# Attention of a hybrid backbone block: head loop rewritten as slots in a fixed order, with side work in a list of jobs

## The chip, the cores and the metric

The kernel runs on one core of a Trainium2 chip. The metric is the device time of one execution in microseconds, the median of the runs. The engines of the core are named as the profile names them: PE (matrix multiplies), PEld (its weight loads), DVE (vector), ACT (scalar), POOL (GpSimd), SP (issues the DMAs).

## The reference, cut to what matters

Two streams, 512 latent tokens `x` and 256 context tokens `ctx`, pass through two layers with shared weights; width is 1024, the FFN is 2816 wide. Layer 0 mixes by differential attention, layer 1 by a gated short convolution; each layer ends in a SwiGLU FFN. Only the latent stream is returned, so the context stream is needed in layer 0 alone, as keys and values. What the change touches is the attention:

```python
def diff_attention(h, hc, wqkv, lam, subln_g, wo, cos, sin, layer_idx, need_ctx):
    # 8 heads; each has two maps of 64 channels (q, k) and 128 value channels
    q, k, v = project(h)
    q, k = apply_rope_2d(q, cos, sin), apply_rope_2d(k, cos, sin)
    qc, kc, vc = project(hc)
    k_all, v_all = concat(kc, k), concat(vc, v)          # 768 keys
    s = einsum('bqhmd,bkhmd->bhmqk', qb, k_all) * 64 ** -0.5
    p = softmax(s)                                        # for each map m
    p = p[:, :, 0] - lam_full * p[:, :, 1]
    o = einsum('bhqk,bkhe->bqhe', p, v_all)
    return (rmsnorm(o, subln_g) * (1 - lam_init)).reshape(B, n, D_MODEL) @ wo
```

around it stand `x + g1 * y` with the gate `g1` from `silu(c) @ ada_w[i] + ada_b[i]`, and the FFN `x + g2 * swiglu(modulate(rmsnorm(x), sh2, sc2))`.

## The kernel before

All operands of a multiply are split in a high and a low part (`split`, L53: ACT writes the rounded part, DVE the rest), and a product is three matmuls on PE: high by high, high by low, low by high (`mm3`, L77 to L80). A weight block is loaded by SP into `raw`, split into `whi`/`wlo` (`load_w`, L64), and then used.

The kernel has an opening stage (norm of the inputs, adaLN of the first sub-layer, and the projections of head 0, ending at about 87 us), attention with its output projection (to 437 us), the FFN of layer 0, the convolution, and the FFN of layer 1. The order on each engine comes from a planner (`schedule_with_timeline_sim`) which moves instructions ahead of others by modelled times; the program gives the dependences.

In attention, `finish_q` and `finish_k` (L442, L451) turn a projection into operands. `rope` (L418) copies PSUM to SBUF on ACT, shuffles on DVE, and does two products and a sum on POOL (for head 0 on DVE). The result is split into `qt`/`kt`, and `halves_to` (L432) moves the halves by eight DMAs a head through SP, so that `ks[m]` holds the high part of 64 channels on partitions 0 to 63 and the low part on 64 to 127, and `qs[m]` the high (or low) part twice. One matmul of 128 rows then gives two of the partial products at once, and two passes give four.

`attend` (L508) goes over a head's four query blocks of 128. For each it computes scores of both maps (`S`, L528: for each map two 512-wide and two 256-wide matmuls), the row maximum on DVE (L532), the exponential on ACT (L536), mixes the maps on DVE (L546), transposes the 768 probabilities on PE (`pt`, L551) and splits them (`pth`, `ptl`). After two blocks the product with the values (`po`, 18 matmuls of 256 columns) follows. `subnorm` (L567) is the norm of a head's output, with its square and its diagonal tiles on POOL. The other work of the loop comes from lists: `proj_qk_steps` and `proj_v_steps` (projections of the next heads), `ada_steps` (L361: the gate and shifts of later sub-layers; ACT scales a 128x1024 block, POOL adds it, L374), and `wo_steps` (L649: output projection of the first `NA` = 5 heads, `poa`). After the loop `wo_rest` (L674) adds the other 3 heads (`pob`) for each half of the tokens, `norm_half` makes the FFN's input, and FFN matmuls (`pa`) begin.

PSUM: two `S` tiles of 1024 columns, two `acc` tiles (projections) and two `pt` tiles (transposes, values, norms).

Of the kernel before, what the change touches and what calls it, by code (L numbers as in the profile page):

```python
# [11 lines left out]
F32 = mybir.dt.float32  # L12
# [7 lines left out]
EPS = 1e-6  # L20
LAM_INIT = 0.8 - 0.6 * math.exp(-0.3 * 0)
# [3 lines left out]
def block_kernel(  # L25
# [87 lines left out]
    early = ("ada", "araw", "qt", "kt", "rcos", "rsin", "sw", "rt")  # L113
# [7 lines left out]
    for tag, n, bufs in (  # L121
        [(f"Or{h}", 512, 1) for h in range(NH)] + [("qs0", 1024, 2), ("qs1", 1024, 2)]
        + [("e", 768, 3), ("pth", 768, 3), ("ptl", 768, 3), ("ks0", 768, 2), ("ks1", 768, 2)]
        + [(f"v{p}{t}", 256, 2) for t in range(KB) for p in "hl"]
        + [("sq", 512, 1), ("dg0", 512, 1), ("dg1", 512, 1)]
        + [(t, 4, 2) for t in ("sv", "sr", "rh", "rl")] + [(t, 4, 3) for t in ("rr", "mx")] + [("ss", 8, 2), ("den", 8, 2)]
        + [("ld", 2, 1)]
        + [("araw", 1024, 2), ("ada", 1024, 1), ("qt", 1024, 1), ("kt", 1536, 1), ("rcos", 512, 1), ("rsin", 512, 1)]
        + [("sw", 512, 1), ("rt", 512, 2)]
    ):  # L130
        ap.tile([P, n], F32, tag=tag, bufs=bufs, name=f"place_{tag}")
# [7 lines left out]
    st1, st2 = (ap.tile([P, P], F32, tag=t, name=n) for t, n in (("ks1", "st1"), ("ks1", "st2")))  # L139
# [20 lines left out]
    def nat(src, t, tag, bufs, name):  # L160
# [6 lines left out]
          for t, (tag, bufs) in enumerate((("ada", 1), ("qt", 1), ("qs0", 2), ("qs0", 2)))]  # L167
    raws0.append(load_ada0(0, 1))
    cn = [nat(ctx, t, "qs1", 2, f"cn{t}") for t in range(CB)]
# [37 lines left out]
    def nat_rstd(src, tag, name):  # L207
# [16 lines left out]
        o = ap.tile([P, 512], F32, tag=tag, bufs=2 if tag == "ks0" else 1, name=f"rs{name}")[:, :nb * P]  # L224
# [51 lines left out]
    rc = nat_rstd(cn, "ks0", "c")  # L276
# [14 lines left out]
    for k in range(DB):  # L291
        raws = raws0 if k == 0 else [load_ada0(k, hf) for hf in range(2)]
        raw = ap.tile([P, 512], F32, tag="e", bufs=3, name=f"raw_w0_{k}")
# [31 lines left out]
    nc.sync.dma_start(rsin, rope_sin)  # L325
# [35 lines left out]
    def ada_steps(l, j, pool, ps_pool, spread_sum):  # L361

        acc = pool.tile([P, D], F32, tag="ada", bufs=1, name=f"ada{l}_{j}")
        for k in range(DB):
            raw = pool.tile([P, D], F32, tag="araw", name=f"araw{l}_{j}_{k}")
            nc.sync.dma_start(raw, ada_w[l, k * P:(k + 1) * P, j * D:(j + 1) * D])
            s = sil[:, 0, k:k + 1]
            if not spread_sum:
# [3 lines left out]
                else:  # L372
                    nc.scalar.activation(raw, raw, AF.Copy, scale=s)
                    nc.gpsimd.tensor_tensor(acc, acc, raw, op=ALU.add)  # L374
# [7 lines left out]
        if not spread_sum:  # L382
            ps = ps_pool.tile([P, 512], F32, tag="acc", name=f"pada{l}_{j}")[:, :DB]
# [32 lines left out]
    SWAP = [i ^ 16 for i in range(32)]  # L416
# [24 lines left out]

    def finish_q(h, ps):  # L442

        r = rope(ps, HD ** -0.5, f"q{h}")
        qt = ap.tile([P, 2, T], F32R, tag="qt", bufs=1, name=f"qt{h}")
        split(qt[:, 0, :], qt[:, 1, :], r)
        q = [ap.tile([P, 2, T], F32R, tag=f"qs{m}", name=f"qs{h}_{m}") for m in range(2)]
        halves_to(q, qt, True)
        return q

    def finish_k(h, ps, psc):  # L451

        r = rope(ps, None, f"k{h}")
        kt = ap.tile([P, 2, KV], F32R, tag="kt", bufs=1, name=f"kt{h}")
        split(kt[:, 0, T:], kt[:, 1, T:], psc)
        split(kt[:, 0, :T], kt[:, 1, :T], r)
        ks = [ap.tile([P, KV], F32R, tag=f"ks{m}", name=f"ks{h}_{m}") for m in range(2)]
        halves_to(ks, kt, False)
        return ks

    def finish_v(g, t, ps):
        vh = ap.tile([P, 256], F32R, tag=f"vh{t}", name=f"vh{g}_{t}")
        vl = ap.tile([P, 256], F32R, tag=f"vl{t}", name=f"vl{g}_{t}")
        split(vh, vl, ps)
        return vh, vl

    def v_load(g):
        cols = slice(2 * D + 256 * g, 2 * D + 256 * (g + 1))
        return [load_w(da_wqkv[0, a * 512:(a + 1) * 512, cols], f"wv{g}_{a}") for a in range(2)]

    def v_tile(g, t, ws):
        src, o = (hx, t * P) if t < TB else (hc, (t - TB) * P)
        ps = psB.tile([P, 512], F32, tag="acc", name=f"psv{g}_{t}")[:, :256]
        for k in range(DB):
            wh, wl = ws[k // 4]
            mm3(
                ps, src[k][0][:, o:o + P], src[k][1][:, o:o + P], wh[:, k % 4, :], wl[:, k % 4, :],
                k == 0, k == DB - 1,
            )
        return finish_v(g, t, ps)  # L480

    V, Q, K = {}, {}, {}
    XT, O = [], []
    NA = NH - 3

    def proj_qk_steps(h):
        wq = load_w(da_wqkv[0, :, P * h:P * (h + 1)], f"wq{h}")
        yield
        wk = load_w(da_wqkv[0, :, D + P * h:D + P * (h + 1)], f"wk{h}")
        ps = psB.tile([P, 512], F32, tag="acc", name=f"psq{h}")  # L490
        gemm_block(ps, [wq], hx)
        Q[h] = finish_q(h, ps)
        yield
        ps = psB.tile([P, 512], F32, tag="acc", name=f"psk{h}")
        gemm_block(ps, [wk], hx)
        psc = psB.tile([P, 512], F32, tag="acc", name=f"pskc{h}")[:, :C]
        gemm_block(psc, [wk], hc)
        K[h] = finish_k(h, ps, psc)
        yield

    def proj_v_steps(g, ts):
        ws = v_load(g)
        yield
        for t in ts:
            V.setdefault(g, []).append(v_tile(g, t, ws))
            yield

    def attend(h, between, after=None):  # L508
        q, ks, vs = Q[h], K[h], V[h // 2]
        vc = slice((h % 2) * P, (h % 2) * P + P)  # L510
        O = ap.tile([P, T], F32, tag=f"Or{h}", bufs=1, name=f"O{h}")
        den = ap.tile([P, 2, TB], F32, tag="den", name=f"den{h}")
        for pr in range(2):
            pts = []
            for kh in range(2):
                pts.append(
                    (ap.tile([P, 3, 256], F32R, tag="pth", bufs=3, name=f"pth{h}_{pr}_{kh}"),
                     ap.tile([P, 3, 256], F32R, tag="ptl", bufs=3, name=f"ptl{h}_{pr}_{kh}"))
                )
            for s in range(2):  # L520
                qb = 2 * pr + s
# [439 lines left out]
```

## Time and profile before

| | |
|---|---|
| Median of 3 runs | 1371.86 us (1370.03 to 1374.06) |
| Profiled execution: own time, span | 1369.84 us, 1368.1 us |
| PE busy over the span | 1312.1 us (96%) |
| DVE, ACT, POOL busy | 780.4, 529.6, 244.8 us |
| Opening stage, 0 to 87 us: PE busy | 67.0 us |
| Attention, 87 to 437 us: PE, DVE busy | 325.6 us, 271.1 us |
| Rest, 437 to 1368 us: PE busy | 919.5 us of 931 |

PE's busy time counts a matmul from its start to its modelled end, and consecutive matmuls overlap, so the distance from one start to the next tells what a matmul costs in a stream. The clock column of a window is the granted clock of PE as a share of full speed (2.4 GHz); it has two levels, 1.0 and 0.5.

### The profile page before, as it was taken

How to read it: one execution, taken by the hardware profiler on the slowest of the kernel's cores; microseconds unless marked ns; L12 is line 12 of the kernel's file. 1: busy time of each engine (PE TensorE's matmuls, PEld its weight loads, DVE VectorE, ACT ScalarE, POOL GpSimd, SP SyncE). 2: the span in 40 equal slices, each digit the busy share in tenths (PEclk: the TensorE clock that was granted, in tenths of full speed). 3: DMA queues.
4: the chain of work that ended last, by engine and by line, in shares of the span. 5: the costliest groups of instructions: out<-in, count | busy, mean ns of one | idle time of the engine just before them, and what ended most of it. 6: DMA issues, size and time to landing. Idle time of an engine off the chain costs nothing.

```text
span 1368.1 us, 18008 instructions
## 1 busy us (share of the span) xinstructions
PE 1312.1 (96%) x7052; PEld 1128.1 (82%) x7052; DVE 780.4 (57%) x1043; ACT 529.6 (39%) x872; POOL 244.8 (18%) x197
## 2 busy tenths in 40 slices
PE   6889899899999999999999999999999999999997
PEld 4678799798888988888888889888988888888887
DVE  6886976777886766776753255444473333332322
ACT  6655646454555432333222244222362232232222
POOL 3244635524314100000001041000340000000000
PEclk9999999999999999999999999999999999999999
DMA  8957633623432666666643333333333333333321
GB/s 291 271 151 219 189 101 124 152 80 93 135 97 80 197 206 200 219 222 203 212 128 96 100 93 93 93 98 88 92 93 99 102 92 93 106 91 109 94 78 62
DMA packets 238742, 182.79 MB, mean 134 GB/s; under 512 B 6937, under 2 KB 220226, under 8 KB 238658
## 3 DMA queue, kind: packets, MB, share of 16 engines
q1 hardware_dynamic: 238658, 181.65, 44.7%
q8 instruction: 55, 0.90, 0.3%
q14 instruction: 29, 0.24, 0.1%
HBM read 162.75 MB, written 4.19 MB: 122 GB/s over the span
## 4 chain that ended last, share of the span: by engine, by line
PE 79%; DVE 8%; DMA 4%; ACT 4%; issue 2%; POOL 2%; SPq 0%; DVEq 0%; ACTq 0%; POOLq 0%
PE po_fo L78 6%; PE po_fo L79 6%; PE po_fo L80 6%; PE pb L79 5%; PE pb L78 5%; PE pb L80 5%; PE pa L78 5%; PE pa L79 5%; PE pa L80 5%; DMA araw<-in_ada_w_dram 3%; PE S L528 2%; PE psc L79 1%; PE psb L80 1%; PE psu L80 1%; PE psc L80 1%
## 5 line engine op out<-in xcount | busy, mean ns | idle before, releaser
L54 ACT CAST whi_f<-raw_f 128x1024 fp32r<-128x1024 f32 x87 | 91.4, 1051 | 234.6 <-issue 117.9
L55 DVE TENSOR_TENSOR wlo_f<-raw_f,whi_f 128x1024 fp32r<-128x1024 f32 x87 | 107.4, 1234 | 79.2 <-ACT whi_f L54 76.2
L55 DVE TENSOR_TENSOR wlo_fo<-raw_fo,whi_fo 128x1024 fp32r<-128x1024 f32 (+1 forms) x48 | 54.5, 1135 | 118.4 <-ACT whi_fo L54 116.8
L607 POOL TENSOR_TENSOR nacc<-nacc,nsq 128x256 f32<-128x256 f32 x30 | 30.7, 1023 | 494.1 <-ACT nsq L603 493.6
L78 PE MATMUL po_fo<-uh,whi_fo 128*128 128x512 f32 (+1 forms) x324 | 118.8, 367 | 0.1
L79 PE MATMUL po_fo<-ul,whi_fo 128*128 128x512 f32 (+1 forms) x324 | 118.7, 366 | 0.0
L80 PE MATMUL po_fo<-uh,wlo_fo 128*128 128x512 f32 (+1 forms) x324 | 118.6, 366 | 0.0
L54 ACT CAST whi_fo<-raw_fo 128x1024 fp32r<-128x1024 f32 (+1 forms) x48 | 47.1, 981 | 177.6 <-PE po_fo L79 146.9
L378 DVE SCALAR_TENSOR_TENSOR ada<-araw,sil,ada 128x1024 f32<-128x1024 f32 x49 | 62.9, 1284 | 39.0 <-DMA araw<-in_ada_w_dram 38.7
L803 DVE TENSOR_TENSOR uu<-sl,pb 128x512 f32<-128x512 f32 (+1 forms) x48 | 30.7, 640 | 81.5 <-PE pb L80 77.2
L536 ACT ACTIVATE e<-S,mx 128x768 f32<-128x768 f32 x64 | 57.8, 904 | 46.7 <-DVE mx L532 36.1
L80 PE MATMUL pb<-h2h,wlo_f 128*128 128x512 f32 (+1 forms) x192 | 71.8, 374 | 0.0
L78 PE MATMUL pa<-h3h,whi_f 128*128 128x512 f32 (+1 forms) x192 | 71.6, 374 | 0.0
L79 PE MATMUL pb<-h2l,whi_f 128*128 128x512 f32 (+1 forms) x192 | 71.5, 372 | 0.0
L78 PE MATMUL pb<-h2h,whi_f 128*128 128x512 f32 (+1 forms) x192 | 71.4, 372 | 0.0
L78 PE MATMUL pb<-h3h,whi_f 128*128 128x512 f32 (+1 forms) x192 | 71.4, 372 | 0.0
L79 PE MATMUL pb<-h3l,whi_f 128*128 128x512 f32 (+1 forms) x192 | 71.4, 372 | 0.0
L80 PE MATMUL pa<-h3h,wlo_f 128*128 128x512 f32 (+1 forms) x192 | 71.4, 372 | 0.0
L80 PE MATMUL pb<-h3h,wlo_f 128*128 128x512 f32 (+1 forms) x192 | 71.4, 372 | 0.0
L79 PE MATMUL pa<-h3l,whi_f 128*128 128x512 f32 (+1 forms) x192 | 71.2, 372 | 0.0
L78 PEld LDWEIGHTS po_fo<-uh,whi_fo 128*128 128x128 f32 x324 | 61.2, 189 | 10.1 <-DVE on L890 0.3
L79 PEld LDWEIGHTS po_fo<-ul,whi_fo 128*128 128x128 f32 x324 | 61.1, 189 | 9.9
(362 smaller groups left out, 3715.2 us busy)
## 6 DMA issues: line engine op xcount, KB each, us to landing
raw_f<-in_ffn_w_in_dram SPq DMA_DIRECT2D x88, 512.0 KB, 3.6
araw<-in_ada_w_dram SPq DMA_DIRECT2D x80, 512.0 KB, 4.4
raw_fo<-in_ffn_w_out_dram SPq DMA_DIRECT2D x32, 512.0 KB, 3.7
raw_a<-in_ada_w_dram SPq DMA_DIRECT2D x32, 256.0 KB, 4.6
qs<-qt SPq DMA_DIRECT2D x32, 256.0 KB, 4.9
raw_wv<-in_da_wqkv_dram SPq DMA_DIRECT2D x12, 512.0 KB, 5.0
ks<-kt SPq DMA_DIRECT2D x32, 192.0 KB, 4.8
raw_fo<-in_ffn_w_out_dram SPq DMA_DIRECT2D x16, 384.0 KB, 4.0
```

The costliest lines, as they stand in the source:

```text
L54: nc.scalar.copy(hi, src)
L55: nc.vector.tensor_tensor(lo, src, hi.bitcast(F32), op=ALU.subtract)
L78: nc.tensor.matmul(ps, sh, mh, start=start, stop=False)
L79: nc.tensor.matmul(ps, sh, ml, start=False, stop=False)
L80: nc.tensor.matmul(ps, sl, mh, start=False, stop=stop)
L378: nc.vector.scalar_tensor_tensor(acc, raw, s, acc, op0=ALU.mult, op1=ALU.add)
L528: nc.tensor.matmul(S[:, a:b], q[m][:, j, qb * P:(qb + 1) * P], ks[m][:, a:b], start=(j == 0), stop=(j == 1),)
L536: nc.scalar.activation(em, S[:, :KV], AF.Exp, bias=mx[:, m:m + 1], accum_out=den[:, m, qb:qb + 1])
L607: nc.gpsimd.tensor_tensor(acc, acc, sq, op=ALU.add)
L803: nc.vector.tensor_tensor(u, s, pb, op=ALU.mult)
```

## The change

Order. PE, DVE, ACT and POOL get a fixed order from the end of the opening stage to the end of the first half of `pob`: what the program says in sequence is what each engine does in sequence (`manual_schedule`). The unit is a slot, one query block of one head; there are 32. In slot i: maxima and exponentials of i, side work, transposes of block i - 1, the mix of i, side work, every second slot the values product, then the scores of block i + 1. `fill(us)` issues that much PE work from one list (`beside_softmax`: 17 projection tasks, then 8 tasks of the output projection); `spot(dve, act)` issues stages of waiting jobs (rope, splits) up to that much time on each engine. A job whose result is needed is issued in full at that point (`finish`).

Scores. The DMAs of `halves_to` are gone. Each map's 64 channels stay where the projection left them, map 0 on partitions 0 to 63 and map 1 on 64 to 127, and scores are three matmuls of 64 rows for each map and width, the two maps in turn: 12 matmuls a block instead of 8.

Rope. Four DVE operations that read PSUM (the sine table is shuffled once ahead), none on ACT or POOL.

Others. POOL's additions in `ada_steps` are halved in width, and the block is fetched a step ahead; the square in `subnorm` goes from POOL to ACT; `NA` is 6; before the first scores four stretches of projections of head 1 are issued; `sqrt_ahead` comes after the fixed part.

```diff
-    nc.sync.dma_start(rsin, rope_sin)
+    rsw = ap.tile([P, T], F32, tag="sw", name="rsw", bufs=1)
+    nc.sync.dma_start(rsw, rope_sin)
+    nc.vector.stream_shuffle(rsin, rsw, SWAP)
...
+                    for hf in range(2):
+                        cs = slice(hf * 512, hf * 512 + 512)
+                        nc.gpsimd.tensor_tensor(acc[:, cs], acc[:, cs], raw[:, cs], op=ALU.add)
...
-    def rope(ps, scale, name):
-        eng = nc.vector if name in ("q0", "k0") else nc.gpsimd
-        r = ap.tile([P, T], F32, tag="rt", name=f"rt{name}")
-        s = ap.tile([P, T], F32, tag="sw", bufs=1, name=f"sw{name}")
-        if scale is None:
-            nc.scalar.copy(r, ps)
-        else:
-            nc.scalar.activation(r, ps, AF.Copy, scale=scale)
-        nc.vector.stream_shuffle(s, r, SWAP)
-        eng.tensor_tensor(r, r, rcos, op=ALU.mult)
-        eng.tensor_tensor(s, s, rsin, op=ALU.mult)
-        eng.tensor_tensor(r, r, s, op=ALU.add)
-        return r
...
-    def halves_to(dst, src, both):
-        for m in range(2):
-            s = src[64 * m:64 * m + 64]
-            for d in range(2):
-                o = dst[m][64 * d:64 * d + 64]
-                nc.sync.dma_start(
-                    o.bitcast(F32), (s if both else s[:, d, :]).bitcast(F32)
-                )
...
+    class Job:
...
+        def finish(self, left=0):
+            while len(self.stages) > left:
+                self.step()
+    def spot(*room):
+        room = list(room)
+        for job in list(jobs):
+            eng = job.stages[0][0]
+            while job.stages and job.stages[0][0] == eng and room[eng] > 0.1:
+                room[eng] -= job.stages[0][1]
+                job.step()
+    def split_stages(hi, lo, src, us):
+        get = src if callable(src) else lambda: src
+        return [
+            (ACT, us, lambda: nc.scalar.copy(hi, get())),
+            (DVE, us, lambda: nc.vector.tensor_tensor(lo, get(), hi.bitcast(F32), op=ALU.subtract)),
...
+    def acc_tile(name):
+        if len(taken) > 1:
+            job, left = taken[-2]
+            job.finish(left)
+        taken.append(None)
+        return psB.tile([P, 512], F32, tag="acc", name=name)
...
+    def rope(ps, name):
+        made = {}
+        def first():
+            for job in ropes[:-1]:
+                job.finish()
+            del ropes[:-1]
+            ropes.append(made["job"])
+            made["r"] = ap.tile([P, T], F32, tag="rt", name=f"rt{name}")
+            made["b"] = ap.tile([P, T], F32, tag="sw", bufs=1, name=f"sw{name}")
+            nc.vector.tensor_tensor(made["b"], ps, rsin, op=ALU.mult)
+        def shuffle():
+            made["t"] = ap.tile([P, T], F32, tag="tmp", bufs=1, name=f"tmp{name}")
+            nc.vector.stream_shuffle(made["t"], made["b"], SWAP)
+        return made, [
+            (DVE, 0.7, first),
+            (DVE, 0.7, lambda: nc.vector.tensor_tensor(made["r"], ps, rcos, op=ALU.mult)),
+            (DVE, 0.75, shuffle),
+            (DVE, 0.7, lambda: nc.vector.tensor_tensor(made["r"], made["r"], made["t"], op=ALU.add)),
...
+        made["job"] = done_q[h] = Job(stages + [
+            (ACT, 0.6, lambda: nc.scalar.activation(hi, made["r"], AF.Copy, scale=HD ** -0.5)),
+            (DVE, 0.9, lambda: nc.vector.scalar_tensor_tensor(
+                lo, made["r"], HD ** -0.5, hi.bitcast(F32), op0=ALU.mult, op1=ALU.subtract)),
+        ])
...
+    WIDE, NARROW = 0.68, 0.36
+    def task_k(h):
+        def run(ws):
+            wh, wl = ws[0]
+            ps = acc_tile(f"psk{h}")
+            for k in range(DB):
+                mm3(ps, wh[:, k, :], wl[:, k, :], *hx[k], k == 0, k == DB - 1)
+                yield WIDE
+            read_by(job_k(h, ps), 4)
+            psc = acc_tile(f"pskc{h}")[:, :C]
+            for k in range(DB):
+                mm3(psc, wh[:, k, :], wl[:, k, :], *hc[k], k == 0, k == DB - 1)
+                yield NARROW
+            read_by(job_kc(h, psc), 0)
...
+        fetch(0)
+        fetch(1)
+        begin_split(0)
+        for n, (_, run) in enumerate(tasks):
+            job, ws = ready.pop(n)
+            job.finish()
+            begin_split(n + 1)
+            fetch(n + 2)
+            yield from run(ws)
...
+    def scores(i):
+        h, qb = divmod(i, TB)
+        begun.add(h)
+        out = [psB.tile([P, 1024], F32, tag="S", name=f"S{h}_{qb}_{m}") for m in range(2)]
+        for a, b in ((0, 512), (512, KV)):
+            for j, (jq, jk) in enumerate(((0, 0), (0, 1), (1, 0))):
+                for m in range(2):
+                    r = slice(64 * m, 64 * m + 64)
+                    nc.tensor.matmul(
+                        out[m][:, a:b], Q[h][r, jq, qb * P:(qb + 1) * P], K[h][r, jk, a:b],
+                        start=(j == 0), stop=(j == 2),
+                    )
+        return out
...
+        nc.scalar.activation(sq, O, AF.Square)
+        yield
...
+    beside_softmax = in_turn(
+        [task_k(1), task_q(1), task_v(1), task_k(2), task_q(2), task_k(3), task_q(3), task_v(2), task_k(4), task_q(4),
+         task_k(5), task_q(5), task_k(6), task_q(6), task_v(3), task_k(7), task_q(7)]
+        + [task_wo(k) for k in range(DB)] + [task_wob()]
+    )
...
+    def fill(us):
+        nonlocal owed
+        owed += us
+        while owed > 0:
+            got = next(beside_softmax, None)
+            if got is None:
+                owed = 0.0
+                return
+            owed -= got
...
+    with tc.manual_schedule(engines={
...
+        taken += [(job_q(0, qps), 4), (job_k(0, kps), 4)]
+        job_kc(0, kcps)
+        for t in range(KB):
+            job_v(0, t, vps[t // TB][:, (t % TB) * 256:(t % TB + 1) * 256])
+        for _ in range(4):
+            fill(3.0)
+            spot(2.8, 2.0)
+        for job in done_k[0] + [done_q[0]] + done_v[0]:
+            job.finish()
+        S, e, ready = scores(0), None, None
+        for i in range(NH * TB):
...
+            part = 2.5 if h < NH - 1 else 2.2
...
+            mix = soften(i, S)
+            spot(1.2, 0.4)
+            fill(part)
+            if i:
+                turn(i - 1, e)
+                if qb % 2 == 0:
+                    ready = divmod((i - 1) // 2, 2)
+            e = mix()
             next(adas, None)
...
+            spot(3.4, 3.6)
+            fill(part)
+            one_step()
+            if h == NH - 1:
+                one_step()
+            if ready:
+                values(*ready)
+                after_values(*ready)
+                ready = None
+            if i + 1 < NH * TB:
+                hn = (i + 1) // TB
+                while hn not in done_q:
...
+                for job in done_k[hn] + [done_q[hn]]:
+                    job.finish()
...
+                S = scores(i + 1)
+        fill(2.5)
+        turn(NH * TB - 1, e)
+        one_step()
+        spot(3.0, 3.0)
+        fill(2.0)
+        one_step()
+        values(NH - 1, 1)
+        after_values(NH - 1, 1)
+        fill(100)
...
+        split_out(NH - 2, 0, T).finish()
+        while len(later) > 1:
+            one_step()
+        for k in range(0, DB, 2):
+            one_step()
+            for kk in (k, k + 1):
+                wo_block(psB, kk, *halves[0])
+        while later:
+            one_step()
...
+    sqrt_ahead(0)
```

## Rows read from the trace of the kernel before

**Rows 1.** Page of the profile: span, and busy time with share and instructions of each engine.

```profile
span 1368.1 us, 18008 instructions
...
PE 1312.1 (96%) x7052; PEld 1128.1 (82%) x7052; DVE 780.4 (57%) x1043; ACT 529.6 (39%) x872; POOL 244.8 (18%) x197
```

**Rows 2.** Windows by stage: PE, PEld, DVE, ACT, POOL busy us (x), clock, DMA share, GB/s.

```profile
60.00:87.00 27.00, 23.27 (x145) 19.84 (x143) 21.21 (x31) 14.34 (x22) 11.86 (x5) 0.87 0.65 203
87.00:108.00 21.00, 17.21 (x94) 14.34 (x93) 16.59 (x22) 10.09 (x17) 13.82 (x7) 1.00 0.54 148
108.00:405.00 297.00, 279.36 (x1763) 252.02 (x1764) 231.88 (x366) 160.28 (x307) 125.35 (x82) 0.97 0.47 131
405.00:437.00 32.00, 29.01 (x218) 26.74 (x216) 22.59 (x45) 16.22 (x36) 14.91 (x21) 1.00 0.26 83
```

**Rows 3.** Timeline of PE in a dense stretch: start us, us, engine, line, operation, tiles.

```profile
268.82 0.39 PE L79 MATMUL psk<-hl,whi_wk 128*128 128x512 f32 x1
269.04 0.40 PE L80 MATMUL psk<-hh,wlo_wk 128*128 128x512 f32 x1
269.28 0.49 PE L551 MATMUL pt<-ident,e 128*128 128x128 f32 x3
269.52 0.48 PE L78 MATMUL psk<-hh,whi_wk 128*128 128x512 f32 x1
...
271.13 0.86 PE L528 MATMUL S<-ks,qs 128*128 128x512 f32 x4
271.83 0.28 PE L79 MATMUL pskc<-cl,whi_wk 128*128 128x256 f32 x1
271.95 0.28 PE L80 MATMUL pskc<-ch,wlo_wk 128*128 128x256 f32 x1
```

**Rows 4.** Groups of DVE, 108 to 405 us: count, busy, mean ns, idle before, releaser.

```profile
L532 DVE TENSOR_REDUCE mx<-S 128x1 f32<-128x768 f32 x64 | 60.2, 948 | 13.9 <-PE S L528 13.8
L546 DVE SCALAR_TENSOR_TENSOR e<-e,rr,e 128x768 f32<-128x768 f32 x31 | 40.7, 1312 | 0.6
L55 DVE TENSOR_TENSOR ptl<-pt,pth 128x384 fp32r<-128x384 f32 x60 | 32.2, 549 | 11.7 <-ACT pth L54 11.7
...
L55 DVE TENSOR_TENSOR wlo_wq<-raw_wq,whi_wq 128x1024 fp32r<-128x1024 f32 x5 | 10.3, 2053 | 0.4 <-ACT whi_wq L54 0.4
...
L55 DVE TENSOR_TENSOR wlo_wk<-raw_wk,whi_wk 128x1024 fp32r<-128x1024 f32 x6 | 7.3, 1223 | 4.3 <-ACT whi_wk L54 4.3
...
L426 DVE STREAM_SHUFFLE swk<-rtk 128x512 f32<-128x512 f32 x7 | 5.2, 743 | 0.0
```

**Rows 5.** Groups of ACT in the same stretch, same columns.

```profile
L536 ACT ACTIVATE e<-S,mx 128x768 f32<-128x768 f32 x64 | 57.8, 904 | 46.7 <-DVE mx L532 36.1 <-DVE e L546 9.8 <-DVE vl L55 0.4
L54 ACT CAST pth<-pt 128x384 fp32r<-128x384 f32 x60 | 28.2, 480 | 30.8 <-PE pt L551 30.3
...
L536 ACT ACTIVATION_READ_ACCUMULATOR e<-S,mx 128x1 f32 x64 | 12.6, 197 | 0.0
```

**Rows 6.** Timeline of DVE, then POOL, at the end of the opening stage.

```profile
64.52 2.88 DVE L230 SCALAR_TENSOR_TENSOR na<-XT,A,rsx 128x512 f32<-128x512 f32 x1
...
71.40 0.75 DVE L230 SCALAR_TENSOR_TENSOR na<-XT,A,rsx 128x512 f32<-128x512 f32 x1
...
85.91 0.42 DVE L55 TENSOR_TENSOR vl<-vps,vh 128x256 fp32r<-128x256 f32 x1 [4.62 <-ACT vh L54]
...
89.95 0.68 DVE L428 TENSOR_TENSOR swq<-swq,rsin 128x512 f32<-128x512 f32 x1
...
63.50 3.34 POOL L374 TENSOR_TENSOR ada<-ada,araw 128x1024 f32<-128x1024 f32 x1 [0.46 <-ACT araw L373]
```

**Rows 7.** Waits, 108 to 405 us: waiter <- releaser, us in total, times, longest.

```profile
PE psv L78 <- DVE kt L55: 5.7, 1, 5.7
```

**Rows 8.** Timeline of all engines: end of attention, first FFN matmul.

```profile
425.71 0.48 DVE L640 SCALAR_TENSOR_TENSOR XR<-pob,mod,XR 128x256 f32<-128x256 f32 x1 [0.60 <-PE pob L80]
...
437.27 0.47 PE L78 MATMUL pa<-h2h,win 128*128 128x256 f32 x1
```

More of the change, by code (lines that the diff above doesn't have):

```diff
@@ L20 @@
 EPS = 1e-6
+SWAP = [i ^ 16 for i in range(32)]
 LAM_INIT = 0.8 - 0.6 * math.exp(-0.3 * 0)
@@ L451, in finish_k, with __init__, step @@
[L451 to L461, printed above, removed]
+    DVE, ACT = 0, 1
+    jobs = []
+    class Job:
+        def __init__(self, stages, after=None):
+            self.stages, self.after = list(stages), after
+            jobs.append(self)
+        def step(self):
+            self.stages.pop(0)[2]()
+            if not self.stages:
+                jobs.remove(self)
+                if self.after:
+                    self.after()
+        def finish(self, left=0):
+            while len(self.stages) > left:
+                self.step()
@@ new lines, in block_kernel, with read_by @@
+    taken = []
+    def acc_tile(name):
[4 more added lines that the diff above has]
+        return psB.tile([P, 512], F32, tag="acc", name=name)
+    def read_by(job, left):
+        taken[-1] = (job, left)
+    ropes = []
+    def rope(ps, name):
[16 more added lines that the diff above has]
+            (DVE, 0.7, lambda: nc.vector.tensor_tensor(made["r"], made["r"], made["t"], op=ALU.add)),
+        ]
@@ new lines, in job_q @@
+    def job_q(h, ps):
+        q = ap.tile([P, 2, T], F32R, tag="q", name=f"q{h}")
+        made, stages = rope(ps, f"q{h}")
+        hi, lo = q[:, 0, :], q[:, 1, :]
+        Q[h] = q
+        made["job"] = done_q[h] = Job(stages + [
[3 more added lines that the diff above has]
+        ])
+        return done_q[h]
@@ L672, in block_kernel, with split_out, task_wo, run @@
-    wob = []
+    split_o = {}
+    def split_out(h, a, b):
+        return Job(split_stages(O[h][0][:, a:b], O[h][1][:, a:b], On[h][:, a:b], 0.7 * (b - a) / T))
+    def task_wo(k):
+        def run(ws):
+            if k == 0:
+                h_pool.release()
+                for nm in ("xtp", "op"):
+                    pools.append(tc.alloc_tile_pool(name=nm, bufs=1, side="right", reuse_waits="tile"))
+                for b in range(DB):
+                    XT.append(pools[0].tile([P, T], F32, name=f"XR{b}"))
+                    nc.sync.dma_start(XT[b], xt_dram[b])
+                for h in range(NH):
+                    O.append(pair(pools[1], h, f"o{h}"))
+            wh, wl = ws[0]
+            ps = acc_tile(f"poa{k}")
+            for h in range(NA):
+                while h not in normed_heads:
+                    yield None
+                for ahead in (h, h + 1):
+                    if ahead < NA and ahead in normed_heads and ahead not in split_o:
+                        split_o[ahead] = split_out(ahead, 0, T)
+                split_o[h].finish()
+                mm3(ps, wh[:, h, :], wl[:, h, :], *O[h], h == 0, h == NA - 1)
+                yield WIDE
+            read_by(Job([(DVE, 0.75, lambda: residual(ps, k, 0, 2, 0, T))]), 0)
+        return lambda: [fetch_w(da_wo[0, :NA * P, P * k:P * (k + 1)], f"woa{k}")], run
@@ L674, in wo_rest, with task_wob, run, wo_block @@
+    wob = []
+    def task_wob():
+        def run(ws):
+            wob.extend(ws)
+            yield 0.0
+        return lambda: [fetch_w(da_wo[0, h * P:(h + 1) * P, :], f"wob{h}") for h in range(NA, NH)], run
+    def wo_block(pool, k, a, b):
+        cs = slice(k * P, (k + 1) * P)
+        ps = pool.tile([P, 512], F32, tag="acc", name=f"pob{k}_{a}")[:, :b - a]
+        gemm_block(ps, [(wh[:, :, cs], wl[:, :, cs]) for wh, wl in wob], cut(O[NA:], a, b))
+        residual(ps, k, 0, 2, a, b)
     def wo_rest(pool, a, b):
@@ L727, in block_kernel, with one_step @@
-    for _ in wo:
-        pass
+            wo_block(pool, k, a, b)
+    done = object()
+    later = []
+    def one_step():
+        if later and next(later[0], done) is done:
+            later.pop(0)
+    beside_softmax = in_turn(
+        [task_k(1), task_q(1), task_v(1), task_k(2), task_q(2), task_k(3), task_q(3), task_v(2), task_k(4), task_q(4),
+         task_k(5), task_q(5), task_k(6), task_q(6), task_v(3), task_k(7), task_q(7)]
+        + [task_wo(k) for k in range(DB)] + [task_wob()]
+    )
```

378 lines of the change are left out of this document (192 added, 186 removed).

## The prediction

> **What bounds the kernel now.** I read the page first: PE is busy 96% of the span, DVE 57% [rows 1]. An engine that is busy so long leaves little to win by hiding its waits, so the next question is where the other 4% lie, and whether "busy" means dense there. The windows by stage answer the first [rows 2]: in attention, 87 to 437 us, PE is busy 17.21 + 279.36 + 29.01 = 325.6 us of 350, so 24 us are idle, and the granted clock is 0.97 in the long middle window, so a part of it ran at the lower level. The change leaves what comes after 437 us alone.
>
> The timeline answers the second [rows 3]. A 512-wide matmul starts 0.22 to 0.24 us after the one before it, a 256-wide one after 0.12, three transposes take 0.24 together, and a map's four score matmuls take 0.70 (271.13 to 271.83). With the counts in the code attention's PE work is: 14 projections of q and k of 24 wide matmuls (336 x 0.225 = 76 us), 7 of the context's k (168 x 0.12 = 20), 18 value tiles (432 x 0.12 = 52), scores (64 x 0.70 = 45), transposes (64 x 0.24 = 15), values (288 x 0.12 = 35), output projection (120 x 0.225 + 144 x 0.12 = 44), and for norms and gates 112 matmuls of one column, taken at the 0.12 us of a 256-wide one, and 18 wide ones (17). That is 304 us. Attention takes 350, so 46 us is the most that an order can give back while the work stays the same.
>
> What holds PE up is seen in the groups of DVE and ACT and in the waits. DVE is busy 231.88 of 297 us in the middle window [rows 2], 7.25 us for each of 32 blocks, against 9.28 us that a block takes. Operations with two inputs in SBUF are long there: the mix means 1.31 us, the split of `wq` 2.05 where that of `wk` takes 1.22 [rows 4]. The timeline shows why: one operation of the same form takes 2.88 us at 64.52, while POOL's 3.34 us addition of an adaLN block runs, and 0.75 us at 71.40, without it [rows 6]. What a late DVE costs PE is seen in the waits: `psv` once stands 5.7 us until DVE has split `kt` [rows 7].
>
> **The change, part by part.** *Opening stage.* The planner had put three weight splits (1.22 us each [rows 4]) and two additions of POOL among the last norms of this stage; the addition at 63.50 costs DVE 2.88 - 0.75 = 2.1 us [rows 6]. DVE is busy 21.2 of 27 us in 60 to 87 [rows 2], and its last gap, 4.62 us before 85.91 [rows 6], is a wait for PE after the norms were done, so PE's end was set by DVE. In a fixed order these pieces come after the stage. At most 3.7 + 2 x 2.1 = 7.9 us are won, at least 0 if PE or the loads set the end; I take 5, since the splits can then lie in that 4.62 us gap. **-5.**
>
> *Ahead of the first scores.* Now 87.4 to 108.4 us, filled with projections. Afterwards 12 us of projections are issued beside head 0's work on DVE: two ropes of four operations (0.68 [rows 6], and 0.74 for the shuffle [rows 4]: 2.78 each), three splits of q and k (0.75 twice and 0.42 [rows 6]: 1.9), six of v at 0.42 [rows 6], two weight splits at 1.22: 12.4 us. `acc_tile` makes the first projection wait until DVE has read head 0's q from PSUM, two operations; with that the first scores stand 13.6 us after the stage.
>
> *Scores.* 12 matmuls of 64 rows stand for 8 of 128. No row shows two matmuls side by side. If the maps' pairs share the array, a block costs 3 x (0.225 + 0.12) = 1.04 us; one after another 2.1; now 1.4 [rows 3]. Nothing in these rows speaks for a gain or a loss, so I take 1.4. The Trainium skill (TensorEngine Tiling, Key Properties) says that tiles on different rows run in parallel, and also that a change of tiling mode drains the engine. By the first a block costs 1.04; by the second, with a drain priced by a matmul's 0.39 us less its 0.22 us distance, twice 0.17 is added, and the sum is 1.4 again. By the first alone PE's slot, worked out below, would be 8.1 us; while DVE sets the pace the time is the same. No run here shows either. The 64 DMAs go, and nothing waits for them.
>
> *A slot, on PE.* Scores 1.4, transposes 0.5, values 1.1, side work 180 us less 12 (issued ahead) less 8 (left for the end), over 32: 5.0, norms 0.5: 8.5 us.
>
> *A slot, on DVE.* 7.25 now. Fourteen ropes change one shuffle (0.74) into 2.78 us: +29 us, +0.9 a slot. POOL loses rope's 55 us and the square's 9 of its 125 us [rows 2], and its adaLN additions, halved, hold DVE up half as long. The excess that rows 4 show (the mix 1.31 against 0.95 for the maximum over as many columns, 0.36 x 31 = 11; `wq` 0.83 x 5 = 4; I put the same again for the rest) is an estimated 30 us; I let half of it go, -0.45. This gives 7.7. Then a new wait: DVE's order is two maxima, side work (1.2), the splits of the transposes. These need `pth` of ACT, which stands behind both exponentials and ACT's side work. From the scores' end: two maxima to 2.0 us [rows 4], the second exponential to 2.3 + 1.1 = 3.4, side work 0.4 to 1.0, `pth` 0.48 [rows 5]: the split can start at 4.5 to 5.0, DVE is ready at 3.4. It stands 1.1 to 1.6 us in every slot, where the planner left 11.7 us for 60 splits [rows 4], 0.4 a block. I take 1.4: 9.1 us. So **DVE sets the pace**, and PE waits 0.6 us in each slot, too short to cost the clock. 32 x 9.1 = 291 us.
>
> *The end.* After the last slot PE has 2.5 + 0.5 + 2.0 + 2.2 us, the 8 us left of the list, and 48 matmuls of `pob` for the first half (5.8 us): 21 us. From the last residual of that half to FFN's first matmul it is 437.27 - 425.71 = 11.6 us [rows 8]; the chain (squares, sums, root, norm) stays. With two heads instead of three in `pob` PE has 5.8 us in it instead of 8.6, so more of it is idle, but its length is the chain's. `sqrt_ahead`, now behind the fixed part, puts one more ACT operation ahead of the squares; at 0.2 to 0.9 us [rows 5] I leave it out.
>
> *Sum.* 13.6 + 291 + 21 + 11.6 = 337 us against 437.3 - 87.4 = 350: -13, with the opening -18. The profiled execution took 1369.84 us, its span 1368.1 us; 1369.84 - 18 = 1352. It lies 2 us under the median of the runs, so I predict **1354 us**.
>
> **Rivals.** *PE sets the pace.* If DVE's gap is filled (jobs overshoot their room) or contention with POOL ends, a slot takes PE's 8.5 us: 19 us less, **1335**. For it: DVE's 7.7 us alone are under 8.5. Against it: the wait for `pth` is in the order itself.
>
> *The wait for DVE moves to PE's side list.* Each of 25 tasks begins with `finish` of its weights' splits, and each projection with `finish` of the rope that still holds its PSUM tile; what isn't done then is put at the end of DVE's queue, behind up to 3.4 us of other jobs, and PE stands still. It is the 5.7 us wait of rows 7, made regular. While PE waits, DVE later waits for scores, so both are lost. The break-even is 18/32 = 0.55 us a slot, 0.7 us for a task. At 1.7 us a task a slot is 9.1 + 1.3 us at worst, less what DVE's own lag hides, say 9.9: **1380**, slower. The same point is reached if scores cost 2.1 (PE 9.2, level with DVE).
>
> *Nothing moves.* A slot of 9.5 us, because POOL's additions, now one in every slot, meet DVE as often as before: 1354 + 13 = **1367**, within the 0.3% (4 us) that a measurement can tell from no change.
>
> **How the numbers follow.** DVE's pace, 1345 to 1362: 0.45. PE's pace, 1330 to 1345: 0.22. No change: 0.13. Slower: 0.20. So faster 0.67, same 0.13, slower 0.20. The range leaves out one in ten on each side: from 1334 to 1378, which takes in scores at 1.04 (hidden under DVE) and at 2.1.
>
> **What would show it.** Opening stage: the first projection of head 1 starts near 82 us. Scores: whether pairs of `S` matmuls start together, and a block's twelve take 1.0, 1.4 or 2.1 us. Pace: scores stand 9.1 us apart, DVE waits some 1.4 us a slot for `pth`, PE's longest waits are for exponentials or DVE; at 8.5 us and DVE waiting for scores PE has the pace. Side list: waits of projections for `wlo` or rope over 0.7 us each speak for the slower case. The end: some 11.6 us from the last residual of the first half to `pa`. The prediction is wrong if planner and fixed order interleave at the seams otherwise than the program says, or if work after 437 us changes its length.

## The result, and the profile after

The changed kernel takes **1494.66 us** (median of 4 runs, 1490.4 to 1496.5) against 1370.94 for the kernel before on the same chip: ratio 1.090, 95% interval 1.086 to 1.093. It is slower by 124 us. 1354 was predicted, and the range ended at 1378. The profiled execution's span is 1494.6 us, against 1368.1 [rows 1].

First the page, then the windows by stage (stretch, its length, busy us of PE, PEld, DVE, ACT and POOL with counts, granted clock, DMA share, GB/s). The stages are those of the prediction: end of the opening stage, projections ahead of the first scores, slots, end of attention, all the rest.

```profile
span 1494.6 us, 17969 instructions
...
PE 1355.0 (91%) x7156; PEld 1147.9 (77%) x7156; DVE 782.0 (52%) x1080; ACT 517.8 (35%) x858; POOL 192.1 (13%) x167
```

```profile
60.00:81.40 21.40, 21.36 (x155) 18.61 (x154) 17.48 (x36) 8.98 (x15) 3.13 (x2) 1.00 0.48 151
81.40:94.90 13.50, 12.94 (x69) 10.77 (x68) 12.72 (x25) 6.11 (x13) 0.00 (x0) 1.00 0.14 40
```

```profile
94.90:504.80 409.90, 312.54 (x1875) 266.74 (x1876) 230.88 (x385) 153.67 (x294) 95.31 (x63) 0.87 0.19 59
504.80:562.60 57.80, 44.59 (x242) 36.52 (x239) 33.56 (x58) 22.82 (x47) 13.66 (x19) 0.94 0.28 87
562.60:1494.60 932.00, 920.47 (x4568) 783.35 (x4566) 444.68 (x500) 289.12 (x424) 63.58 (x66) 1.00 0.41 124
```

DVE's work in the slots, 230.88 us, is what it was [rows 2], and no engine is full any more: PE stands still for 97.4 of 409.9 us, DVE for 179. The granted clock of 0.87 means that about a quarter of the stretch ran at 1.2 GHz instead of 2.4. By stage, with each group of scores taken from its first matmul, the 126.5 us between the two spans are:

| stretch | before, us | predicted | after | after less before |
|---|---|---|---|---|
| to the first projection of head 1 | 87.5 | 82 | 81.5 | -6.0 |
| from there to the first scores | 20.9 | 13.6 | 13.4 | -7.5 |
| 31 slots, scores to scores | 290.6 (9.4 each) | 282 (9.1) | 408.5 (13.2) | +117.9 |
| last scores to FFN's first matmul | 38.3 | 41.7 | 59.3 | +21.0 |
| rest | 930.8 | 930.8 | 932.0 | +1.2 |

The waits in the slots say who stands for whom (waiter, line <- releaser, line: us in total, times, longest):

```profile
DVE ptl L56 <- ACT pth L55: 75.4, 29, 6.1
...
DVE mx L670 <- PE S L653: 67.1, 26, 7.0
...
PE psv L79 <- DVE vl L469: 31.4, 12, 4.0
...
PE S L653 <- ACT q L519: 10.3, 2, 6.7
PE psq L79 <- DVE rtk L507: 9.9, 5, 2.6
PE poa L79 <- ACT o L468: 9.6, 3, 3.5
```

DVE waits for PE, PE for DVE, and both for ACT: a ring. One slot shows it, the longest, from scores at 375.54 to the next scores at 398.28 (22.7 us, in which DVE is busy 8.7). PE first, then DVE, then ACT; the columns are start, duration, engine, line, operation, tiles, and in brackets the idle time before it and who ended it.

```profile
375.54 1.33 PE L653 MATMUL S<-k,q 64*128 64x512 f32 x12
...
377.49 0.28 PE L81 MATMUL psv<-whi_wv,hl 128*128 128x256 f32 x1
381.06 0.39 PE L79 MATMUL psv<-whi_wv,hh 128*128 128x256 f32 x1 [3.29 <-DVE vl L469]
...
382.07 0.41 PE L79 MATMUL psv<-whi_wv,hh 128*128 128x256 f32 x1
382.29 0.41 PE L80 MATMUL psv<-wlo_wv,hh 128*128 128x256 f32 x1
...
389.87 0.58 PE L79 MATMUL psv<-whi_wv,hh 128*128 128x256 f32 x1 [3.48 <-DVE vl L469]
```

```profile
376.90 1.82 DVE L670 TENSOR_REDUCE mx<-S 128x1 f32<-128x768 f32 x2 [3.63 <-PE S L653]
378.64 1.22 DVE L469 TENSOR_TENSOR wlo_wk<-raw_wk,whi_wk 128x1024 fp32r<-128x1024 f32 x1
380.58 0.42 DVE L469 TENSOR_TENSOR vl<-psv,vh 128x256 fp32r<-128x256 f32 x1 [0.72 <-ACT vh L468]
385.38 1.05 DVE L56 TENSOR_TENSOR ptl<-pt,pth 128x384 fp32r<-128x384 f32 x2 [4.38 <-ACT pth L55]
...
386.79 1.02 DVE L685 SCALAR_TENSOR_TENSOR e<-e,rr,e 128x768 f32<-128x768 f32 x1
387.73 1.75 DVE L520 SCALAR_TENSOR_TENSOR q<-rtq,q 128x512 fp32r<-128x512 f32 x1
389.40 0.41 DVE L469 TENSOR_TENSOR vl<-psv,vh 128x256 fp32r<-128x256 f32 x1
```

```profile
378.79 0.89 ACT L674 ACTIVATE e<-S,mx 128x768 f32<-128x768 f32 x1
...
379.66 0.62 ACT L519 ACTIVATE q<-rtq 128x512 fp32r<-128x512 f32 x1
380.18 0.37 ACT L468 CAST vh<-psv 128x256 fp32r<-128x256 f32 x1
```

After the scores PE has six matmuls left of a value tile. The next value tile needs one of the two `acc` tiles, and the older is free when DVE has run its `vl`. In the written order that `vl` stands behind the two maxima and a weight split, and its high half `vh` on ACT behind the two exponentials and a part of `q`: PE stands 3.29 us. Then it is DVE that stands: its next instruction, the split of the transposes, waits 4.38 us, because PE does the transposes only after the matmuls that were held up. After that DVE has work for 4 us in a row (387.73: a split of `q` that lasts 1.75 us beside a POOL addition), the next `vl` is behind that, and PE stands 3.48 us. And each of these two pauses is paid twice, as the windows of the same slot show:

```profile
377.60:381.00 3.40, 0.17 (x2) 0.00 (x0) 2.68 (x4) 2.65 (x6) 0.00 (x0) 1.00 0.01 3
381.70:385.00 3.30, 3.30 (x17) 3.30 (x17) 0.00 (x0) 0.13 (x1) 0.00 (x0) 0.50 0.27 80
386.20:389.80 3.60, 0.19 (x2) 0.00 (x0) 3.53 (x7) 0.95 (x2) 2.78 (x2) 0.81 0.00 0
390.00:398.20 8.20, 8.20 (x38) 8.05 (x38) 0.79 (x2) 0.00 (x0) 1.63 (x2) 0.50 0.21 64
```

In the first pause the granted clock is still 1.00; soon after PE works again it is 0.50 (1.2 GHz), and so for all of 390.0 to 398.2 after the second. A 256-wide matmul then starts 0.21 us after the one before it (382.07, 382.29) and not 0.12.

### The profile page after: what moved, and what is told of

Its sections match the earlier page's. It is cut to its first block, busy times and chain, and to the rows that moved or that the text cites. A ratio compares the mean times of both kernels' runs of the same rounds, so it can differ in the third digit from the quotient of the medians.

```text
span 1494.6 us, 17969 instructions
## 1 busy us (share of the span) xinstructions
PE 1355.0 (91%) x7156; PEld 1147.9 (77%) x7156; DVE 782.0 (52%) x1080; ACT 517.8 (35%) x858; POOL 192.1 (13%) x167
## 4 chain that ended last, share of the span: by engine, by line
PE 79%; DVE 11%; ACT 4%; DMA 3%; issue 2%; POOL 1%; SPq 1%; ACTq 0%; DVEq 0%; POOLq 0%
PE po_fo L79 5%; PE pa L80 5%; PE pa L79 5%; PE po_fo L80 5%; PE po_fo L81 5%; PE pa L81 5%; PE pb L80 5%; PE pb L81 5%; PE pb L79 5%; PE S L653 3%; DVE mx L670 2%; ACT e L674 2%; PE psv L79 1%; DVE ptl L56 1%; DVE e L685 1%
## 5 line engine op out<-in xcount | busy, mean ns | idle before, releaser
L391 POOL TENSOR_TENSOR ada<-ada,araw 128x512 f32<-128x512 f32 x42 | 73.0, 1758 | 244.2 <-ACT araw L388 197.2
L670 DVE TENSOR_REDUCE mx<-S 128x1 f32<-128x768 f32 x64 | 58.3, 951 | 71.2 <-PE S L653 71.2
L56 DVE TENSOR_TENSOR ptl<-pt,pth 128x384 fp32r<-128x384 f32 x64 | 33.2, 553 | 86.1 <-ACT pth L55 85.6
```

The costliest lines, as they stand in the source:

```text
L56: nc.vector.tensor_tensor(lo, src, hi.bitcast(F32), op=ALU.subtract)
L391: nc.gpsimd.tensor_tensor(acc[:, cs], acc[:, cs], raw[:, cs], op=ALU.add)
L670: nc.vector.tensor_reduce(out=mx[:, m:m + 1], in_=Ss[m][:, :KV], axis=AX.X, op=ALU.max, negate=True)
```

## The experiments

Three theories. **H** (hand-back): the reads that free an `acc` tile stand late in the written order of DVE and ACT. **O** (order as such): with a written order any wait of one engine reaches all. **W** (work): the changed operations cost more, scores on 64 rows or rope on DVE. Three letters come in further on: **G**, GpSimd's work stretches DVE's, **A**, ScalarE's written order is as bad as VectorE's, and **M**, two written orders are needed for the loss.

For each run of the tables below, the *slots* are the stretch from its first to its last scores: *idle* is its length less PE's busy time, and *clock* is the most that the lower level can cost there, length x (1 - granted clock): a share of 2 x (1 - clock) of the time then does half the work. It is a bound and not the cost, since a part of that time lies in pauses, where PE loses nothing by it; and with the clock given to 0.01 it is known to some 2 us. The kernel before, measured beside each of these runs, took 1368.5 to 1371.4 us (medians); so differences in us between runs of different tables or paragraphs are right to some 3 us, and each ratio is to the kernel before beside it.

**1. The planner back.** All of the change but the written order:

```diff
-    with tc.manual_schedule(engines={PE, DVE, Activation, Pool}):
+    with ExitStack():
```

> The changed kernel with the planner's order in place of the fixed one; scores on 64 rows, rope on DVE, job list and tasks stay. Theory H (hand-back): PE stands still because the operation that frees a PSUM tile has its place in DVE's fixed order behind a slot's softmax; a planner may put it ahead, so the time falls to 1340 to 1375 us. Theory O (order as such): any fixed order ties the four engines to each other's latest wait; same number here. Theory W (work): the new scores and the rope on DVE cost the time themselves; then it stays above 1450 us.

Measured: **1374.97 us**, ratio 1.004 (1.002 to 1.007). The order costs 120 us, and W is out as the cause: the same instructions take some 6 us more than the kernel before beside them (1368.51 us). Its window of the slots:

```profile
94.20:396.30 302.10, 298.90 (x1885) 252.46 (x1885) 227.65 (x395) 152.33 (x291) 67.28 (x55) 0.98 0.25 74
```

PE idles only 3.2 us of 302, but it has more to do: the planner tore the groups of 12 score matmuls apart (8 of 32 are whole). From one start to the next the 384 score matmuls take 62 us there, against 41 us where the groups stayed whole (PE alone in written order, experiment 8).

**2. Scores, one map after the other.** The three products of one map, then those of the other.

```diff
-            for j, (jq, jk) in enumerate(((0, 0), (0, 1), (1, 0))):
-                for m in range(2):
+            for m in range(2):
+                for j, (jq, jk) in enumerate(((0, 0), (0, 1), (1, 0))):
```

> The changed kernel with the score matmuls of map 0 all ahead of those of map 1, so that neighbours use the same 64 rows. If the two maps run side by side in the changed kernel (pairs of starts 3 ns apart in its trace), a block's twelve take 2.0 to 2.1 us instead of 1.2, and as scores lie in the chain of a slot under H and O, the time grows by 32 x 0.8 = 26 us to about 1520 us. If pairing gave nothing, no change.

Measured: 1490.75 us, ratio 1.090 (1.086 to 1.094), as the changed kernel. My expectation missed: the 12 matmuls still take 1.25 us from the first of them to the next tile's first, as in the changed kernel (1.25 us, median).

```profile
94.88 1.32 PE L653 MATMUL S<-k,q 64*128 64x512 f32 x12
96.13 0.50 PE L79 MATMUL psq<-hh,whi_wq 128*128 128x512 f32 x1
```

In the trace they still start in pairs, 10 ns apart (median). So this edit did not make them serial, and the run only shows that the order inside a group is of no account.

**3. Rope as before** (copy on ACT, shuffle on DVE, products and sum on POOL), in the written order. Unlike in the kernel before, head 0's rope is on POOL here too.

> The changed kernel, fixed order kept, with the rope as before the change: copy from PSUM on ACT, shuffle on DVE, two products and the sum on POOL. W: DVE loses about 29 us of work and the time falls by 25 us or more, to 1470 us or less. H and O: DVE has room anyway (56% busy in the loop), so less than 15 us either way; the copy on ACT frees PSUM a little earlier, POOL's slower products come later: 1480 to 1510 us.

Measured: 1500.78 us, ratio 1.097 (1.094 to 1.101). In the slots DVE is relieved of 20 us (210.93 us busy from 103.1 to 508.9), and they get only 4.1 us shorter (405.8 against 409.9), while the first scores come 8.2 us later (103.1 against 94.9); in all nothing is won. DVE's load alone does not set the pace.

**4. Value tiles handed back at once.** The two split stages of a value tile are issued right behind its matmuls instead of whenever the list comes to them.

```diff
-                read_by(job_v(g, t, ps), 0)
+                job = job_v(g, t, ps)
+                job.finish()
+                read_by(job, 0)
```

> The changed kernel, fixed order kept; only the two split stages of a value tile are issued right behind its matmuls, ahead of the next softmax, instead of when room is found or the tile is needed again. H: the 31 us that psv waits for vl go, and with them some of the half-speed clock: 1430 to 1455 us. O: other waits take their place, 1480 to 1500 us. W: no change, 1495 us.

Measured: **1439.1 us**, ratio 1.052 (1.049 to 1.056), 55 us less. The wait of `psv` for `vl` (31.4 us) is gone; what leads now:

```profile
PE S L655 <- ACT q L519: 10.3, 2, 6.6
PE poa L79 <- ACT o L468: 9.6, 3, 3.5
PE psq L79 <- DVE rtk L507: 9.1, 5, 2.7
PE psv L79 <- DVE rtq L507: 4.5, 3, 3.5
```

**5. The products of q and k too.** As 4, and `job.finish(4)` behind each q and k projection, so that the two reads of its PSUM tile come at once.

> Fixed order on all four engines; the value tiles' split stages and the two reads of PSUM of each q and k projection (products with cosines and sines) are issued right behind their matmuls. Theory H: with value tiles alone it was 1439 us with 13.6 us of TensorE waits for q and k products left, which at 2 to 1 (clock) are 15 to 30 us: 1405 to 1425 us. Theory O (what was left in that run is the chain of softmax and the order itself): 1430 to 1445 us.

Measured: 1433.63 us, ratio 1.046 (1.041 to 1.051). Only 5.5 us: less than H said, inside O's band. The `rtk` and `rtq` waits are gone, but others have come up in their place, the first and the third of these rows:

```profile
PE psk L81 <- DVE wlo_wk L469: 9.9, 3, 4.4
PE poa L79 <- ACT o L468: 9.0, 3, 3.5
PE S L661 <- DVE q L522: 4.9, 1, 4.9
```

What is pushed forward in one queue pushes something else back: here, it seems, the splits of the weights, for which `psk` had waited 0.5 us in experiment 4.

**6. Everything early.** As 5; the next task's weights are split four matmul groups into the task before it, and `O` one head further ahead.

```diff
-            yield from run(ws)
+            for m, us in enumerate(run(ws)):
+                if m == 4 and n + 1 in ready:
+                    ready[n + 1][0].finish()
+                yield us
```

> Fixed order on all four engines; besides the hand-backs of value tiles and of q and k products, the splits of the next task's weights are issued four matmul groups into the task before it, and the splits of O one head further ahead. In the run with the hand-backs alone (1434 us) TensorE still waited 17 us for halves of weights, 13 us for halves of O. Theory H (whatever TensorE needs stands late in the written order of VectorE and ScalarE; each wait counts about twice, by the clock): 1385 to 1410 us. Theory O (a written order on all engines loses some 60 us wherever its single steps stand): 1425 to 1440 us.

Measured: 1418.68 us, ratio 1.035 (1.032 to 1.038). Between the two bands. Of 124 us lost, early placing has now won back 76; 47 are left.

**7. GpSimd's additions left out**, from the kernel of 5.

> As the run with all hand-backs early, but GpSimd's additions of the modulation vectors of the first block are left out (the vectors are wrong; ScalarE's scaling and the loads stay): 95 us less GpSimd work beside the attention. Theory G (VectorE's instructions are stretched by GpSimd's, as the 1.75 us q split in the 22.7 us slot, and in a fixed order every stretch reaches TensorE): 15 to 40 us less than that run. Theory O: within 8 us of it.

Measured: 1421.21 us, against 1433.63 for experiment 5, measured beside it: 12.4 us less, just under G's band and above O's. (The additions were 75 us of POOL's time in the slots, 97.3 against 22.4; the expectation's 95 us is all of POOL's work there.) In the slots DVE is busy 214.5 instead of 229.5 us, and the slots are 13.9 us shorter: 15 us off DVE gave 14, although DVE is idle a third of the time. In experiment 3 the slots gave 4 us for 20 of rope's work on DVE. There the work went to ACT and POOL, so it may have stayed in the ring; that was not tested.

**8. Whose order is it?** The changed kernel's text, with different engines in written order, the others by the planner:

> Only TensorE keeps the written order; VectorE, ScalarE and GpSimd are ordered by the planner, all else as in the changed kernel. Theory H (a PSUM tile is handed back late because its reads stand behind the softmax in VectorE's written order): VectorE is free to read earlier, so most of the 120 us go, and the score groups stay whole, which saves the 25 us that the planner alone lost on broken pairs: 1345 to 1385 us. Theory O (TensorE's own written order stalls whatever the others do): still 1440 to 1500 us. Theory M (both orders are needed for the loss): near the planner alone, 1375 us.

> VectorE, ScalarE and GpSimd keep the written order and TensorE is ordered by the planner. Theory H: the hand-back stays where it is, and TensorE can only go round it: 1420 to 1490 us. Theory O: TensorE's order was the fault, so most of the loss goes: 1365 to 1390 us.

> The changed kernel's text; TensorE, ScalarE and GpSimd keep the written order and VectorE alone is ordered by the planner. Theory H (the loss comes through VectorE's written queue: the reads that free a PSUM tile stand behind the softmax there): most of the 120 us go, 1375 to 1400 us. Theory A (ScalarE's written order is as bad, since the high halves go through it ahead of the low ones): 1430 to 1480 us.

> The same text; TensorE and VectorE keep the written order, ScalarE and GpSimd are ordered by the planner. Theory H: the loss stays, 1460 to 1495 us. Theory A: 1375 to 1420 us.

| in written order | us | ratio (95%) | slots | idle | clock |
|---|---|---|---|---|---|
| none (experiment 1) | 1375.0 | 1.004 (1.002 to 1.007) | 302.1 | 3 | 6 |
| PE | 1375.0 | 1.003 (1.001 to 1.005) | 296.0 | 18 | 15 |
| DVE, ACT, POOL | 1418.3 | 1.034 (1.030 to 1.039) | 333.2 | 28 | 23 |
| PE, ACT, POOL | 1445.0 | 1.054 (1.042 to 1.066) | 365.1 | 68 | 37 |
| PE, DVE | 1481.0 | 1.080 (1.075 to 1.086) | 392.0 | 89 | 43 |
| all four | 1494.7 | 1.090 (1.086 to 1.093) | 409.9 | 97 | 53 |
| all four, everything early (6) | 1418.7 | 1.035 (1.032 to 1.038) | 335.6 | 45 | 30 |

PE's order alone costs nothing against the planner: 1375.0 us is M's number and lies in H's band, and O as that expectation puts it, PE's own order stalling whatever the others do, is out. The three others without PE cost 43 us: O's band is missed by far, and H's by 2 us. With PE's order alone its waits in the slots are few and short (2.7 us the longest); the window of its slots, and the largest group of waits:

```profile
96.80:392.80 296.00, 277.65 (x1875) 241.93 (x1876) 220.88 (x392) 149.57 (x290) 63.96 (x52) 0.95 0.24 73
```

```profile
PE spro L753 <- DVE ptl L56: 6.1, 5, 2.1
```

The loss is there where two or more written orders wait for each other, and not with PE's alone: PE's with DVE's +106 us over PE's alone, PE's with ACT's and POOL's +70, and with all three +120, so the two do not add up; either closes the ring. PE's with POOL's, in the slots, adds 3 us (experiment 9). DVE's order alone, ACT's alone and POOL's alone were not run, so it is not shown that one of these by itself would cost nothing. H as I had put it, with DVE at fault, is half right: with DVE free the time was 1445, in A's band and above H's. `vl` is still late, since its high half `vh` stands behind the exponentials on ACT, as the timelines of ACT, DVE and PE around one such wait show below the row of the wait:

```profile
PE psv L79 <- DVE vl L469: 26.7, 11, 4.5
```

```profile
115.43 0.89 ACT L674 ACTIVATE e<-S,mx 128x768 f32<-128x768 f32 x1
116.21 0.20 ACT L674 ACTIVATION_READ_ACCUMULATOR e<-S,mx 128x1 f32 x1
116.30 0.37 ACT L468 CAST vh<-psv 128x256 fp32r<-128x256 f32 x1
```

```profile
116.78 0.42 DVE L469 TENSOR_TENSOR vl<-psv,vh 128x256 fp32r<-128x256 f32 x1
```

```profile
117.25 0.38 PE L79 MATMUL psv<-whi_wv,hh 128*128 128x256 f32 x1 [3.25 <-DVE vl L469]
```

A is half right too: it expected at most 1420 with DVE and PE written, and 1481 was measured.

**9. A version to beat both?** PE alone in written order with the texts of 6 and 5; DVE alone free with the text of 6; PE and POOL written in the slots, with the end left to the planner.

> The same text as the run with everything early, but only TensorE keeps its written order. With the text of the changed kernel that was 1375 us with 18 us of TensorE waits, few of them for what is moved here (3 us for O, 2 us for q). Both theories: 1365 to 1378 us; theory H allows down to 1360.

> The text with the hand-backs alone early, TensorE alone in written order. Where the planner orders VectorE by its own view of when things are ready, the place in the text hardly counts: 1368 to 1380 us, against 1434 us for the same text with four engines in written order.

> The text with hand-backs and splits early; all but VectorE in written order. The modulation vectors are then summed a step a slot and not in bursts as in the run with TensorE alone in written order (two stretches of 14 to 16 us at a clock of 0.81 to 0.88 there): theory H 1360 to 1380 us; theory A 1390 to 1420 us, near the 1419 us of the same text with four written orders.

> The changed kernel's text; TensorE and GpSimd keep the written order in the slots, the stage after the last slot is left to the planner. With TensorE alone in written order it was 1375 us, of which 5 us were TensorE waits in that last stage: 1362 to 1378 us, so at best some 0.5% under the kernel before.

Measured: 1377.06 (1.004), 1374.71 (1.003), 1406.27 (1.026) and 1378.37 us (1.006). The first two are as expected, the third lies in A's band, and the fourth just above its own. None beats the kernel before. The place in the text counts for 76 us when all four orders are written, and for nothing, 1375 to 1377, when the planner orders DVE, ACT and POOL. With DVE alone free, early places won 39 us (1445 to 1406); the 31 us that are then left over PE's order alone, and the 47 us of experiment 6, were not taken apart: they are O's share, or further places that I did not find.

## Why the prediction was wrong

**Opening stage: the number was right**, 82 predicted, 81.5 measured. But PE is now busy 21.36 of the last 21.4 us at a clock of 1.00, where it was 23.27 of 27 at 0.87 [rows 2]; a part of the gain may be the clock, which the prediction did not count. **Ahead of the first scores: right**, 13.6 and 13.4; PE is busy 12.94 of these 13.5 us.

**Scores: right in the sum.** A group of 12 takes 1.26 us from its first matmul to the next tile's (375.54 to 376.80), and the steps at its edges are 0.1 us longer than others of their kind (375.33 to 375.54 and 376.80 to 377.02, where 256-wide ones take 0.12); dense the group would be 6 x about 0.175 = 1.05, so a group costs 1.05 + 0.2 + 0.2 = 1.45 us where I had 1.4. The Trainium skill (TensorEngine Tiling (Array Packing), Key Properties) says that tiles work in parallel, and the trace agrees: the two matmuls of a pair, on different rows, start 3 ns apart (median). The Trainium skill also says there that a change of tiling mode drains the engine. The 0.4 us over 1.05 would be that, 0.2 each way, if nothing else lengthens these steps, which no run here tells apart.

**A slot on PE: the work was right, the wait wrong.** With PE's order alone the slots are 296.0 us; less 18.4 idle and up to 14.8 for the clock that is 8.5 to 9.0 us a slot, where 8.5 was predicted. In the changed kernel PE waits 97.4 / 31 = 3.1 us a slot, where I had 0.6.

**A slot on DVE: the work was right, "DVE sets the pace" wrong.** This is the step that failed. DVE is busy 230.88 / 31 = 7.45 us a slot (predicted 7.7; the mix fell to 1.02 us from the 1.31 of rows 4, while POOL's work in the slots fell to 95 us from 125 [rows 2]). But it waits for `pth` 75.4 / 31 = 2.4 us (predicted 1.4) and for scores 67.1 / 31 = 2.2 us (predicted none). I had found the wait for `pth` in the order, added it to DVE's work, and compared the sum with PE's work as if the two ran side by side, the slot being the larger. They don't run side by side once each has its own fixed order and there are two `acc` tiles between them: part of PE's work comes after a part of DVE's in the same slot, and the other way round, so a slot is a sum around the ring, not a maximum (experiments 4 and 8; a third `acc` tile was not tried). DVE's slot is 7.45 + 2.4 + 2.2 and about 1.1 of smaller waits, 13.2 us.

**The clock: left out.** "Too short to cost the clock" was said of pauses of 0.6 us, and no row showed it. The pauses were up to 6.7 us (for `q`; up to 4.0 for `vl`). The loss over PE's order alone, 409.9 - 296.0 = 114 us, is 97.4 - 18.4 = 79 us more idle time and 312.54 - 277.65 = 35 us more busy time for the same 1875 matmuls. These 35 us are put down to the clock, since the work and its order on PE are the same. So the lower level costs between 35 and 53 us in the slots, against at most 9 before (297 us at 0.97 [rows 2]).

**The rival "the wait for DVE moves to PE's side list"** had the mechanism, the 5.7 us wait of rows 7 made regular, and even the remark that both engines then lose. Its price was wrong: I charged 1.7 us to each of 25 tasks, capped the slot at 9.9 us and gave it 0.20. There is one hand-back for each accumulation tile, and the 18 value tiles, with 24 matmuls of 256 columns each to cover them, were the worst: moving the reads of those alone was worth 55 us. It should have been the forecast.

**The end**: from the last scores 30 us to the last residual of the first half were predicted (a slot of 9.1 and 21), 47.5 were measured (503.35 to 550.85), by the same kind of waits (`ptl` for `pth` 10.2 us in 504.8 to 562.6). From there to the first FFN matmul 11.8 us, predicted 11.6.

**What the change is worth without the loss.** With PE's order alone the first scores stand at 96.8 us, 11.6 earlier than before, but the slots last 3.5 us longer and the end 8.8: 1370.4 against 1368.1 in the profiled executions. The projections that were moved ahead are a gain at the beginning only; the work that would have to close up behind them meets a PE that is already 94% busy.

## What to carry to other kernels

When a planner's order is replaced by a written one on several engines, do not price a loop's turn as the largest of the engines' own sums: write each engine's order in a row, draw who waits for whom, and add up the longest way around, with every PSUM tile that goes back to its writer as an edge. An instruction that frees a buffer belongs right behind what fills it, ahead of work that only has to be done some time. And on a kernel where PE is nearly full, pauses on PE are to be charged with the lower clock that may follow as well: here 97 us of idle time in the slots came with 35 to 53 us of it.

## What the runs showed of the hardware that was not expected

The lower clock can come after a pause and not in it: 1.00 in 377.6 to 381.0, while PE was idle, 0.50 in 381.7 to 385.0, while it was fully busy; in the second pause of that slot, 0.81 on the mean, it came within. Shorter pauses went with it too: with PE's order alone PE stood 2.14 us before 294.39, and the granted clock is 1.00 in 292.4 to 294.3 and 0.50 in 295.0 to 298.2, while it was fully busy. And the order of the matmuls in a group on 64 rows does not matter: three of one map and then three of the other took the same 1.25 us as strict alternation.
